# Rotary sine product moved ahead of the swap of halves, and two S5 tables moved to ScalarE, in a two-layer hybrid encoder

## The chip, the cores and the metric

The program runs on one core of a Trainium2 chip. The metric is the time of one execution on the device in microseconds (us), the median of several runs. TensorE is called PE here as in the profile, VectorE DVE, ScalarE ACT, GpSimd POOL and SyncE SP; SP computes nothing and issues most of the DMAs. PE writes its results to an accumulator memory (PSUM), from which DVE and ACT can read; all else lies in the main on-chip memory (SBUF).

## The reference, cut to what matters

Two layers over 1024 tokens of width 1024, each a mixer and an MLP. The change lies in the first mixer: a combined projection gives queries and keys (4 heads, two halves of 64 each), values, and the input of an S5 layer (32 groups of 16 channels, a complex diagonal state of 64 per group, in both directions). Queries and keys are rotated:

```
def apply_rope(t, cos, sin):
    t1, t2 = jnp.split(t, 2, axis=-1)
    return jnp.concatenate([t1 * cos - t2 * sin, t2 * cos + t1 * sin], axis=-1)
...
    q = apply_rope(split_qk(q), cos, sin) * (ATTN_QK_DIM ** -0.5)
    k = apply_rope(split_qk(k), cos, sin)
```

The S5 layer is a scan over time, whose step for one state is `ar`, `ai`, with the result read out through `c_re`, `c_im`:

```
    elems = (jnp.broadcast_to(ar, bur.shape), jnp.broadcast_to(ai, bur.shape), bur, bui)
    _, _, xr, xi = lax.associative_scan(_complex_affine_combine, elems,
                                        reverse=(direction == 1), axis=1)
```

## The kernel before

Activations lie transposed, 128 channels on the partitions and 1024 tokens along a row. A float32 product is done as three products of split halves (`mm_part`, L133): a tile of a projection is 48 matmuls of 128x512.

The first mixer has three parts in time. First the projections of the S5 input and the S5 parameters. Then, in `s5_main`, eight batches of four groups. Each batch has `s5_gains` (tables: `gtr`, `gti` by DVE and POOL, the rotation `wr`, `wi`, the decay `dec`, a transposed input `U`), `s5_readout` and `s5_kernels` (mostly POOL, ACT and small matmuls, ending in the Toeplitz tile `toep`, which eight DMAs spread from `KK`), `s5_states` (matmuls L824 into the accumulator `side`, then sixteen DVE instructions L827 to L853, four of them scans L838 and L841 that read `dec`) and `s5_out` (matmuls L864 to L866). The rotation is an angle in turns `fr` less its nearest whole number, then two sines on ACT: one of `fr` itself (L747) and one of a quarter turn less its absolute value (L748), which DVE takes (L746).

The twelve tiles of queries, keys and values come as "fill": `qk_tile` eight times and `val` four times. In the text of the program they stand behind the loop over the batches. What each engine does first is decided by a planner (`schedule_with_timeline_sim=True`), which orders the instructions of every engine by its own estimate of the times. So the matmuls of the fill lie between those of the batches. Once ordered, each engine works strictly in its order, and so does the DMA queue of SP.

A rotated tile goes through `qk_tile` so: ACT copies the accumulator `ps` with a scale to `raw` (tile `qraw`, L919); four DMAs swap blocks of 32 partitions into `sw` (L923); DVE multiplies `ps` by the cosine into `t` (tile `rot`, L925); POOL multiplies `sw` by the sine (L926); DVE adds (L927); ACT and DVE split the sum into `qh` and `ql` (L108, L109), which DMAs L931 and L932 store to DRAM. The last tile (i = 7) accumulates in `side`, the others in `big`. After the mixer's gated unit (`glu`), the attention loads queries, keys and values back (L957 to L961).

The accumulators are scarce: two `big`, one `side`, one `sm` and one `fill`. PE waits before a matmul until the tile that it overwrites has been read.

Of the kernel before, what the change touches and what calls it, by code (L numbers as in the profile page):

```python
# [13 lines left out]
AF = mybir.ActivationFunctionType  # L14
ALU = mybir.AluOpType
# [12 lines left out]
NB = 4  # L28
# [27 lines left out]
class Trunk:  # L56
# [661 lines left out]
    def s5_gains(self, b, S, pb, u_tok):  # L718

        nc = self.nc  # L720
        v, gp = nc.vector, nc.gpsimd
        gs = slice(NB * b, NB * b + NB)
        N4 = [P, NB, 128]
        GT = [P, NB, 8, 16]
        t0, t1 = (pb.tile(GT, F32, tag=f"tm{k}", name=f"tm{k}") for k in range(2))
        bbr, bbi = (x[:, gs, :].unsqueeze(2).to_broadcast(GT) for x in S["bb"])
        g7r, g7i = (x[:, gs, :].unsqueeze(3).to_broadcast(GT) for x in S["g7"])
        gtr = pb.tile(GT, F32, tag="gtr", name="gtr")
        gti = pb.tile(GT, F32, tag="gti", name="gti")
        self.cmul(gtr, gti, g7r, g7i, bbr, bbi, t0, t1, v, gp)  # L730
        G = []
        for j, src in enumerate((gtr, gti)):
            ps = self.small()
            for g in range(NB):
                nc.tensor.transpose(ps[:, 128 * g : 128 * g + 128], src[:, g].rearrange("p s m -> p (s m)"), self.ident)
            t = pb.tile(N4, F32, tag=f"G{j}", name=f"G{j}")
            nc.scalar.copy(t, ps.rearrange("p (g k) -> p g k", g=NB))
            G.append(t)

        tn = wr = pb.tile(N4, F32, tag="wr", name="wr", bufs=2)  # L740
        fr = wi = pb.tile(N4, F32, tag="wi", name="wi", bufs=2)
        for g in range(NB):
            nc.scalar.activation(fr[:, g], S["count"], AF.Copy, scale=S["psi"][:, NB * b + g : NB * b + g + 1])
        v.tensor_scalar(tn, fr, MAGIC, MAGIC, ALU.add, ALU.subtract)
        v.tensor_tensor(fr, fr, tn, ALU.subtract)
        v.scalar_tensor_tensor(tn, fr, -1.0, fr, ALU.mult, ALU.max)  # L746
        nc.scalar.activation(wi, fr, AF.Sin, scale=TURN)  # L747
        nc.scalar.activation(wr, tn, AF.Sin, scale=-TURN, bias=S["quarter"])  # L748
        dec = pb.tile(N4, F32, tag="dec", name="dec")
        gp.tensor_tensor(  # L750
            dec, S["edge"].unsqueeze(1).to_broadcast(N4), S["rho"][:, gs].unsqueeze(2).to_broadcast(N4), ALU.mult
        )
        U = pb.tile(N4, F32, tag="U", name="U", bufs=2)
        ps = self.small()
        for g in range(NB):
            o = 512 * (b % 2) + 128 * g
            nc.tensor.transpose(ps[:, 128 * g : 128 * g + 128], u_tok[:, b // 2, o : o + 128], self.ident)
        nc.scalar.copy(U, ps.rearrange("p (g c) -> p g c", g=NB))
        return dict(U=U, G=G, w=(wr, wi), dec=dec)
# [153 lines left out]
    def qk_tile(self, i, xg, pr, cosr, sinr, dst, last):  # L913

        nc = self.nc
        ps = self.proj(self.load_w(W_QK + i), xg, self.side() if last else None)
        raw = pr.tile([P, SEQ], F32, tag="qraw", name="qraw")
        scale = -0.125 if i % 2 == 0 else 1.0
        nc.scalar.activation(raw, ps, AF.Copy, scale=scale)  # L919
        sw = pr.tile([P, SEQ], F32, tag="sw", name="sw")  # L920
        for a in range(4):
            b = a ^ 1
            nc.sync.dma_start(sw[32 * a : 32 * a + 32], raw[32 * b : 32 * b + 32])  # L923
        t = pr.tile([P, SEQ], F32, tag="rot", name="rot")
        nc.vector.scalar_tensor_tensor(t, ps, scale, cosr, ALU.mult, ALU.mult)  # L925
        nc.gpsimd.tensor_tensor(sw, sw, sinr, ALU.mult)  # L926
        nc.vector.tensor_tensor(t, t, sw, ALU.add)  # L927
        hi = pr.tile([P, SEQ], F32R, tag="qraw", name="qh")
        lo = pr.tile([P, SEQ], F32R, tag="sw", name="ql")
        self.split(hi, lo, t)  # L930
        nc.sync.dma_start(dst[0], hi.bitcast(F32))  # L931
        nc.sync.dma_start(dst[1], lo.bitcast(F32))  # L932
# [581 lines left out]
def layout(i):  # L1514
    a = lambda k: np.asarray(i[k])
    mt = lambda w: w.reshape(8, 128, -1, 128).transpose(2, 1, 0, 3).reshape(-1, 128, 1024)

    def pairs(w, nk):
        m = w.reshape(-1, nk, 128, w.shape[1] // 256, 2, 128)
        return m.transpose(0, 3, 2, 4, 1, 5).reshape(-1, 128, 2 * nk * 128)  # L1520

    def blocks(w, ks, ms):

        t = w.reshape(-1, 128, w.shape[1] // 128, 128)
        return np.stack([t[k, :, m].transpose(1, 0, 2).reshape(128, -1) for m in ms for k in ks])

    halves = (list(range(4)), list(range(4, 8)))
    ffs = {}
    for l in range(2):
        win, wout = a("w_ff_in")[l], a("w_ff_out")[l]  # L1530
        ffs[f"win{l}"] = np.stack([blocks(win, halves, (2 * j, 2 * j + 1)) for j in range(16)])

        npairs = 16 - 2 * l
        parts = []
        for u in range(1, npairs + 4):
            rows = [[2 * j + f for j in range(max(0, u - 4), min(npairs, u))] for f in range(2)]
            q = (u - npairs) % 4
            parts.append(blocks(wout, rows, (q, q + 4)).ravel())
        ffs[f"wout{l}"] = np.concatenate(parts)
    ffs["wtail"] = np.stack([blocks(a("w_ff_out")[1], ([28, 29, 30, 31],), (d,))[0] for d in range(8)])  # L1540

    we = mt(a("w_in_even")[0])
    wqk = np.stack([we[0:4], we[4:8]], 1).reshape(8, 128, 1024)
    wo = mt(a("w_in_odd")[0]).reshape(5, 8, 128, 1024)
    odd = []
    for h in range(8):
        odd += [wo[0, h], wo[2, h], wo[3, h], wo[1, h], wo[4, h]]
    oo = a("w_out_odd")[0].reshape(8, 128, 1024)
    two = oo[5:7].reshape(2, 128, 8, 128)[:, :, PAIRED].reshape(2, 128, 2, 4, 128).transpose(2, 1, 3, 0, 4).reshape(2, 128, 1024)
    oo = np.concatenate([oo[:5], two, oo[7:]])  # L1550
    woe = a("w_out_even")[0]
    apart = woe[:512].reshape(4, 128, 2, 4, 128).transpose(3, 1, 2, 0, 4).reshape(4, 128, 1024)
    w = np.concatenate([
        we[12:16], wqk, we[8:12], pairs(a("s5_w_glu")[0], 4), apart, pairs(woe[512:], 4), np.stack(odd), oo,
    ])
    col = lambda v: v.reshape(-1, 128).T
    vec = np.concatenate([
        col(a("norm_mix_g")), col(a("norm_mlp_g")), col(a("final_norm_g")), col(a("hgrn_norm_g")),
        col(a("hgrn_lb_logits")), col(a("s5_b_glu")), col(a("diff_subln_g")),
    ], axis=1)  # L1560
    vec = np.concatenate([vec, np.zeros((128, 80 - vec.shape[1]), np.float32)], axis=1)
    up = np.triu(np.ones((128, 128), np.float32))
    consts = np.concatenate([np.eye(128, dtype=np.float32), up, up.T, np.tile(np.arange(128, dtype=np.float32), (128, 1))], axis=1)
    x = a("x")[0].T.reshape(8, 128, 1024)
    gp = lambda v: v.transpose(0, 2, 1).reshape(128, 32)
    step = np.broadcast_to(a("s5_log_step")[0][:, :, None], (2, 32, 64))
    s5_par = np.stack([gp(a("s5_lam_re")[0]), gp(a("s5_lam_im")[0]), gp(step)], 1)
    gpm = lambda v: v.transpose(0, 2, 1, 3).reshape(128, 32, 16)
    s5_b = np.stack([gpm(a("s5_b_re")[0]), gpm(a("s5_b_im")[0])], 1)
    gpn = lambda v: v.transpose(0, 3, 1, 2).reshape(128, 32, 16)  # L1570
    s5_c = np.stack([gpn(a("s5_c_re")[0]), gpn(a("s5_c_im")[0])], 1)
    inv = 10000.0 ** (-np.arange(0, 64, 2, dtype=np.float32) / np.float32(64.0))
    ang = np.arange(SEQ, dtype=np.float32)[None, :] * inv.astype(np.float32)[:, None]
    cos, sin = np.cos(ang).astype(np.float32), np.sin(ang).astype(np.float32)
    cos = np.tile(cos, (4, 1))
    sin = np.tile(np.concatenate([-sin, sin]), (2, 1))
    lam = np.broadcast_to(a("diff_lambda")[0], (128, 4, 64))
    s5_d = a("s5_d")[0].reshape(32, 16).T
    return {"w": w, "vec": vec, "consts": consts, "x": x, "s5_par": s5_par, "s5_b": s5_b, "s5_c": s5_c, "s5_d": s5_d,
            "cos": cos, "sin": sin, "lam": lam, **ffs}  # L1580
# [18 lines left out]
```

## Time and profile before

| What | Value |
|---|---|
| median of 3 runs | 2706.62 us (2703.37, 2706.62, 3588.91) |
| the profiled execution | 2711.57 us, its span 2709.7 us |
| granted PE clock, mean of the span | 0.97 |
| PE busy | 2511.2 us (93%) |
| DVE busy | 2021.5 us (75%) |
| ACT busy | 1055.7 us (39%) |
| POOL busy | 920.9 us (34%) |

The profiled execution is 4.95 us above the median, and 1.87 us of it lie outside its span. PE's busy share is high nearly everywhere; the stretches in which it is not are few, and the one that the change touches lies between 60 and 375 us.

### The profile page before, as it was taken

To read this page: it belongs to the slowest core of one execution; us is meant where nothing else is said; L and a number is where in the kernel's file an instruction comes from. 1 tells how busy PE (TensorE), PEld (TensorE's weight loads), DVE (VectorE), ACT (ScalarE), POOL (GpSimd) and SP (SyncE) were. 2 spreads that over 40 slices of the span, in tenths; PEclk is the share of its full clock that TensorE was granted. 3 is DMA by queue.
4 is the path that set the end of the run, shared out by engine and by line. 5 is a ranking of instruction groups with operands and counts; after the bars stand their busy time and mean duration, and the time that the engine had idled before them with its cause. 6 is when DMAs were issued, how large, how long until landed. Compare 5 with 4: busy or idle time off the path is not lost.

```text
span 2709.7 us, 33309 instructions
## 1 busy us (share of the span) xinstructions
PE 2511.2 (93%) x12040; PEld 2074.6 (77%) x12040; DVE 2021.5 (75%) x2896; ACT 1055.7 (39%) x1911; POOL 920.9 (34%) x732
## 2 busy tenths in 40 slices
PE   6888889998999989999799999999978999899987
PEld 5767768886788867777688888888857888678776
DVE  9688867868667678887876766666677676688867
ACT  3333346665334344444421222222254343444434
POOL 6455421213332334453222222222223323344422
PEclk9898999998999989999899999999989999999999
DMA  3122362302334356666111111111122343466672
GB/s 145 59 77 79 128 179 63 90 28 98 96 113 127 103 150 147 161 172 172 37 45 39 40 40 39 40 39 40 51 78 75 114 124 114 135 152 170 149 190 75
DMA packets 135253, 269.02 MB, mean 99 GB/s; under 512 B 16432, under 2 KB 29360, under 8 KB 135088
## 3 DMA queue, kind: packets, MB, share of 16 engines
q1 hardware_dynamic: 118384, 236.47, 27.2%
q0 software_dynamic: 16704, 30.42, 7.2%
q8 instruction: 95, 1.56, 0.2%
q14 instruction: 70, 0.57, 0.1%
HBM read 173.50 MB, written 87.03 MB: 96 GB/s over the span
## 4 chain that ended last, share of the span: by engine, by line
PE 57%; DVE 22%; DMA 8%; issue 7%; ACT 2%; POOL 2%; SPq 1%; POOLq 0%; DVEq 0%; ACTq 0%
PE big L133 21%; PE b L352 10%; PE c L352 6%; PE a L352 6%; DMA z<-sq 5%; DVE wl L109 4%; DVE l L109 3%; PE sm L1010 2%; PE sm L133 1%; PE big L1379 1%; PE tail L542 1%; ACT h L108 1%; PE big L975 1%; PE sm L1335 1%; PE big L1350 1%
## 5 line engine op out<-in xcount | busy, mean ns | idle before, releaser
L133 PE MATMUL big<-hi,wh 128*128 128x512 f32 x976 | 310.1, 398 | 13.7 <-ACT hi L111 12.1
L133 PE MATMUL big<-lo,wh 128*128 128x512 f32 x976 | 308.2, 395 | 9.7 <-DVE lo L112 9.7
L133 PE MATMUL big<-hi,wl 128*128 128x512 f32 x976 | 307.3, 395 | 0.0
L352 PE MATMUL b<-h,wh 128*128 128x512 f32 x672 | 270.4, 402 | 30.2 <-DVE w L362 23.6
L352 PE MATMUL b<-h,wl 128*128 128x512 f32 x672 | 267.1, 398 | 2.5 <-DVE wl L109 2.5
L352 PE MATMUL b<-l,wh 128*128 128x512 f32 x672 | 266.8, 397 | 0.3 <-DVE l L109 0.3
L108 ACT CAST wh<-s 128x512 fp32r<-128x512 f32 (+3 forms) x204 | 118.6, 583 | 343.5 <-PE b L352 170.0
L109 DVE TENSOR_TENSOR l<-z,h 128x512 fp32r<-128x512 f32 x232 | 196.0, 873 | 75.2 <-ACT h L108 74.8
L109 POOL TENSOR_TENSOR wl<-raw,wh 128x1024 fp32r<-128x1024 f32 x58 | 143.0, 2466 | 317.1 <-ACT wh L108 308.3
L108 ACT CAST wh<-raw 128x1024 fp32r<-128x1024 f32 x74 | 77.5, 1047 | 436.0 <-PE big L133 295.6
L133 PEld LDWEIGHTS big<-lo,wh 128*128 128x128 f32 x976 | 184.6, 190 | 49.7 <-DVE lo L112 11.0
L133 PEld LDWEIGHTS big<-hi,wh 128*128 128x128 f32 x976 | 182.2, 190 | 52.5 <-ACT hi L111 12.8
L109 DVE TENSOR_TENSOR wl<-r,wh 128x512 fp32r<-128x512 f32 (+3 forms) x279 | 215.5, 780 | 8.7 <-ACT wh L108 8.6
L133 PEld LDWEIGHTS big<-hi,wl 128*128 128x128 f32 x976 | 184.7, 190 | 38.5 <-issue 0.2
L108 ACT CAST h<-z 128x512 fp32r<-128x512 f32 x232 | 139.3, 618 | 179.3 <-DMA z<-sq 76.0
L108 ACT CAST wh<-r 128x512 fp32r<-128x512 f32 (+3 forms) x279 | 158.7, 581 | 99.6 <-PE b L352 46.5
L352 PE MATMUL a<-h,wh 128*128 128x512 f32 x448 | 178.1, 398 | 14.1 <-ACT wh L108 7.5
L352 PE MATMUL c<-h,wh 128*128 128x512 f32 x448 | 177.4, 396 | 10.2 <-ACT h L108 7.8
L326 POOL TENSOR_TENSOR s<-s,r 128x512 f32<-128x512 f32 (+3 forms) x68 | 98.6, 1450 | 252.0 <-DVE wl L109 251.0
L333 POOL TENSOR_TENSOR s<-s,r 128x512 f32<-128x512 f32 (+3 forms) x68 | 89.9, 1323 | 273.2 <-DVE wl L109 224.2
L352 PE MATMUL a<-h,wl 128*128 128x512 f32 x448 | 177.1, 395 | 5.3 <-DVE wl L109 5.3
L352 PEld LDWEIGHTS b<-h,wh 128*128 128x128 f32 x672 | 128.6, 191 | 68.9 <-DVE w L362 33.5
(438 smaller groups left out, 6025.4 us busy)
## 6 DMA issues: line engine op xcount, KB each, us to landing
raw<-w SPq DMA_DIRECT2D x74, 512.0 KB, 3.3
r<-win SPq DMA_DIRECT2D x128, 256.0 KB, 3.0
sq<-z SPq DMA_DIRECT2D x128, 256.0 KB, 3.0
z<-sq SPq DMA_DIRECT2D x128, 256.0 KB, 4.9
xd<-z POOLq DMA_DIRECT2D x116, 256.0 KB, 5.8
r<-wout SPq DMA_DIRECT2D x96, 256.0 KB, 4.6
x<-x SPq DMA_DIRECT2D x16, 512.0 KB, 7.6
xd<-x SPq DMA_DIRECT2D x32, 256.0 KB, 2.3
```

The costliest lines, as they stand in the source:

```text
L108: nc.scalar.copy(hi, src)
L109: (eng or nc.vector).tensor_tensor(lo, src, hi, ALU.subtract)
L133: nc.tensor.matmul(ps[:, t], a[:, s], b[:, t], start=(first and i == 0 and j == 0), stop=(last and i == n - 1 and j == 2),)
L326: gp.tensor_tensor(s2, s1, r["r11"], ALU.add)
L333: gp.tensor_tensor(s2, s2, r["r12"], ALU.add)
L352: nc.tensor.matmul(bank[p], x[:, s], y, start=(p in (1, 6, 5) and i == 0 and j == 0), stop=(i == n - 1 and j == 2), skip_group_check=True,)
L542: nc.tensor.matmul(ps, x[:, ks], y, start=(k == 0 and j == 0), stop=(k == 3 and j == 2))
L975: nc.tensor.matmul(S[:, ks], qa[:, qs], kk[:, ks], start=True, stop=False)
L1010: nc.tensor.matmul(po, wT[:, k, :], A["V"][:, k, :], start=(k == 0), stop=(k == NT - 1))
L1335: nc.tensor.matmul(ps[:, 128 * b : 128 * b + 128], ki[:, bs], qd[:, bs], start=True, stop=True)
L1350: nc.tensor.matmul(kv[:, bs], kTs[d][:, bs], V[:, bs], start=True, stop=True)
L1379: nc.tensor.matmul(po[:, bs], l, r, start=(i == 0), stop=(i == len(terms) - 1))
```

## The change

In `s5_gains` the absolute value moves from DVE (L746) to ACT, and the decay table `dec` from POOL (L750) to ACT, where it becomes four instructions of 128 columns. In `qk_tile` the product with the sine is taken from the accumulator by DVE, ahead of the swap, in place of ACT's copy; POOL's product behind the swap goes. The host's sine table has its signs exchanged to fit.

```diff
@@ s5_gains
-        v.scalar_tensor_tensor(tn, fr, -1.0, fr, ALU.mult, ALU.max)
+        nc.scalar.activation(tn, fr, AF.Abs)
...
-        gp.tensor_tensor(
-            dec, S["edge"].unsqueeze(1).to_broadcast(N4), S["rho"][:, gs].unsqueeze(2).to_broadcast(N4), ALU.mult
-        )
+        for g in range(NB):
+            nc.scalar.activation(dec[:, g], S["edge"], AF.Copy, scale=S["rho"][:, NB * b + g : NB * b + g + 1])
@@ qk_tile
-        nc.scalar.activation(raw, ps, AF.Copy, scale=scale)
+        nc.vector.scalar_tensor_tensor(raw, ps, scale, sinr, ALU.mult, ALU.mult)
...
         nc.vector.scalar_tensor_tensor(t, ps, scale, cosr, ALU.mult, ALU.mult)
-        nc.gpsimd.tensor_tensor(sw, sw, sinr, ALU.mult)
         nc.vector.tensor_tensor(t, t, sw, ALU.add)
@@ layout
-    sin = np.tile(np.concatenate([-sin, sin]), (2, 1))
+    sin = np.tile(np.concatenate([sin, -sin]), (2, 1))
```

The planner sees other instructions and orders the first mixer with its attention anew, and a short piece of the first MLP. Below, the line numbers of the changed kernel are 1 less than before from L754 to L925 and 2 less from L927 on; its new instructions are L746 (absolute value), L751 (decay) and L918 (sine product).

DVE around the seventh rotated tile, before: the tile's product and sum (L925, L927) stand behind the end of a batch, next to each other.

```order
L853 TENSOR_TENSOR z_1711<-z_1711,z_1710 128x512
L852 TENSOR_TENSOR z_1709<-z_1709,z_1712 128x512
L925 SCALAR_TENSOR_TENSOR rot<-big,cosr 128x1024
L927 TENSOR_TENSOR rot<-rot,sw 128x1024
L804 TENSOR_TENSOR d_1813<-d_1813,side 16x64
L806 TENSOR_TENSOR KK<-d_1813,d_1814 16x4x16
L109 TENSOR_TENSOR ql<-rot,qh 128x1024
```

The same tile on DVE after:

```order
L805 TENSOR_TENSOR KK<-d_1692,d_1693 16x4x16
L744 TENSOR_SCALAR wr<-wi 128x512
L745 TENSOR_TENSOR wi<-wi,wr 128x512
L918 SCALAR_TENSOR_TENSOR qraw<-big,sinr 128x1024
L924 SCALAR_TENSOR_TENSOR rot<-big,cosr 128x1024
L109 TENSOR_TENSOR wl<-raw,wh 128x1024
L826 TENSOR_TENSOR z_1730<-side,wr 128x512
L827 TENSOR_TENSOR z_1731<-side,wi 128x512
L828 TENSOR_TENSOR z_1732<-side,wr 128x512
L829 TENSOR_TENSOR z_1733<-side,wi 128x512
L775 SCALAR_TENSOR_TENSOR hi<-hi,tm_1814 128x640
L925 TENSOR_TENSOR rot<-rot,sw 128x1024
```

The sum (now L925) has moved away from the two products, behind a weight split and the first four instructions of the next batch; the end of the batch before it (`KK`) stands three rows ahead of the products.

The DMA queue of SP ahead of that tile's swap, before: the swap stands behind the store of a value tile.

```order
L809 DMA toep<-KK 16x4x128 x8
L116 DMA raw<-w 128x1024
L1133 DMA dv_123<-vtok 128x1024
L923 DMA sw<-qraw 32x1024 x4
L1478 DMA x_2775<-x 128x1024
```

And after:

```order
L116 DMA raw<-w 128x1024
L1131 DMA dv_123<-vtok 128x1024
L808 DMA toep<-KK 16x4x128 x8
L922 DMA sw<-qraw 32x1024 x4
L116 DMA raw<-w 128x1024
```

The eight Toeplitz DMAs have moved from ahead of a weight load to right ahead of the swap.

ACT in the third batch of tables, before: the copy of `U` stands behind the four angle instructions L743.

```order
L1132 COPY vtok<-fill 128x512
L743 ACTIVATE wi<-count,psi 128x128 x4
L758 COPY U<-sm 128x512
L1132 COPY vtok<-fill 128x512
L747 ACTIVATE wi<-wi 128x512
L748 ACTIVATE wr<-wr,quarter 128x512
```

And after:

```order
L788 COPY bz_800<-bk_600 64x4x16
L1130 COPY vtok<-fill 128x512
L746 ACTIVATE wr<-wi 128x512
L747 ACTIVATE wi<-wi 128x512
L757 COPY U<-sm 128x512
L748 ACTIVATE wr<-wr,quarter 128x512
```

The copy of `U` (now L757) has moved behind the absolute value and the first sine.

## Rows read from the trace of the kernel before

**Rows 1.** Busy time by stretch: span, then PE, PEld, DVE, ACT, POOL, granted clock, DMA.
```profile
100.00:354.00 254.00, 217.78 (x1127) 182.24 (x1125) 218.74 (x224) 88.12 (x158) 135.85 (x110) 0.92 0.31 100
354.00:405.00 51.00, 42.14 (x181) 34.04 (x182) 26.73 (x27) 25.28 (x30) 9.64 (x4) 0.91 0.63 166
405.00:600.00 195.00, 191.47 (x1226) 169.11 (x1226) 146.98 (x235) 128.57 (x288) 37.99 (x36) 1.00 0.24 60
```

**Rows 2.** PE's waits from 100 to 358 us: total us, times, longest.
```profile
PE sm L865 <- DVE z L852: 13.0, 4, 4.5
PE side L824 <- DVE d L804: 10.3, 3, 4.0
PE sm L864 <- ACT U L758: 7.8, 3, 4.1
PE fill L1131 <- DVE rot L1125: 2.3, 1, 2.3
PE side L133 <- DVE z L830: 1.8, 1, 1.8
```

**Rows 3.** Busy time by slices of 10 us around one wait of PE.
```profile
200.00:210.00 10.00, 7.13 (x28) 5.99 (x29) 9.70 (x13) 4.91 (x14) 2.82 (x3) 0.66 0.50 161
210.00:220.00 10.00, 8.91 (x56) 7.58 (x56) 6.42 (x5) 5.48 (x7) 7.33 (x4) 1.00 0.31 105
```

**Rows 4.** DVE by form, 100 to 375 us: busy, mean ns, idle before.
```profile
L927 DVE TENSOR_TENSOR rot<-rot,sw 128x1024 f32<-128x1024 f32 x8 | 11.8, 1469 | 12.4 <-POOL sw L926 9.6 <-DMA toep<-KK 2.7
...
L925 DVE SCALAR_TENSOR_TENSOR rot<-big,cosr 128x1024 f32<-128x1024 f32 x7 | 8.5, 1216 | 3.8 <-ACT qraw L919 3.8
...
L746 DVE SCALAR_TENSOR_TENSOR wr<-wi 128x512 f32<-128x512 f32 x6 | 4.1, 691 | 0.2
```

**Rows 5.** POOL by form, same stretch.
```profile
L926 POOL TENSOR_TENSOR sw<-sw,sinr 128x1024 f32<-128x1024 f32 x8 | 20.5, 2566 | 18.1 <-DMA sw<-qraw 18.1
...
L750 POOL TENSOR_TENSOR dec<-edge,sp 128x512 f32<-128x512 f32 x7 | 9.2, 1313 | 0.6
```

**Rows 6.** DVE in order of time, four pieces: start, us, instruction.
```profile
133.25 1.23 DVE L925 SCALAR_TENSOR_TENSOR rot<-big,cosr 128x1024 f32<-128x1024 f32 x1
...
137.21 2.83 DVE L849 TENSOR_TENSOR z<-z,wr 128x512 f32<-128x512 f32 x1
...
140.10 0.67 DVE L850 TENSOR_TENSOR z<-z,wi 128x512 f32<-128x512 f32 x1
...
283.36 2.88 DVE L610 TENSOR_TENSOR gtr<-g,bbr 128x512 f32<-128x512 f32 x1
...
322.10 1.53 DVE L849 TENSOR_TENSOR z<-z,wr 128x512 f32<-128x512 f32 x1
...
368.72 1.23 DVE L927 TENSOR_TENSOR rot<-rot,sw 128x1024 f32<-128x1024 f32 x1 [3.02 <-POOL sw L926]
```

**Rows 7.** POOL in order of time, first two tiles.
```profile
116.27 2.38 POOL L926 TENSOR_TENSOR sw<-sw,sinr 128x1024 f32<-128x1024 f32 x1 [3.48 <-DMA sw<-qraw]
...
133.45 1.04 POOL L750 TENSOR_TENSOR dec<-edge,sp 128x512 f32<-128x512 f32 x1
...
136.70 2.79 POOL L926 TENSOR_TENSOR sw<-sw,sinr 128x1024 f32<-128x1024 f32 x1
```

**Rows 8.** ACT in order of time, first tile.
```profile
110.87 1.03 ACT L919 ACTIVATE qraw<-big 128x1024 f32<-128x1024 f32 x1 [3.32 <-PE big L133]
```

**Rows 9.** The DMA queue of SP in order of time, sixth tile.
```profile
272.90 5.96 SPq L809 DMA_DIRECT2D toep<-KK  x8
278.98 2.46 SPq L923 DMA_DIRECT2D sw<-qraw  x4
```

**Rows 10.** ACT by form, 100 to 375 us.
```profile
L743 ACT ACTIVATE wi<-count,psi 128x128 f32<-128x128 f32 x24 | 7.7, 389 | 40.2 <-DVE z L851 40.2
...
L747 ACT ACTIVATE wi<-wi 128x512 f32<-128x512 f32 x6 | 3.8, 630 | 4.5 <-DVE wr L746 4.4
```

**Rows 11.** PE in order of time, start of the attention.
```profile
389.45 0.47 PE L975 MATMUL big<-kk,qa 128*128 128x512 f32 x1 [1.81 <-DMA kk<-dk]
```

## The prediction

> **What bounds the kernel now.** I began with the share of busy time by stretch, because an average over 2710 us says little about a change that touches 300 of them. From 100 to 354 us, in which the S5 batches and the fill run together, PE and DVE are each busy 86% of the time (217.8 and 218.7 of 254 us); ACT has 35% and POOL 53% [rows 1]. Behind it, in the attention, PE is busy 98% at full clock. So the stretch to read is the first one, and both of its busy engines count.
>
> Next, PE's waits there. The large ones add up to 35.2 us, of which 27.4 end with DVE (the last instructions of a batch's states, the small sum `d`, a scaled value tile, the reads of `side`) and 7.8 with ACT, a copy of `U` out of the only `sm` accumulator [rows 2]. PE never waits for POOL. What PE waits for is therefore mostly a DVE that comes late, and POOL matters only through DVE.
>
> Each wait has a second price: in the 10 us in which PE waited 4 us, the granted clock was 0.66, and 1.00 in the next [rows 3]. Over the whole stretch it was 0.92 [rows 1], which is 0.08 x 254 = 20 us of work that the lower of the two levels (1.2 against 2.4 GHz) did not do.
>
> POOL reaches DVE in two ways. DVE waited 12.4 us for the sum of the rotation, nearly all of it behind POOL's sine product [rows 4]. And DVE's instructions with two operands in SBUF grow when POOL computes beside them: one that takes 0.67 us took 2.83 beside the 2.79 us sine product, others 2.88 and 1.53 [rows 6, 7]. An instruction with one operand in the accumulator does not grow: the cosine product took 1.23 us beside `dec` [rows 6, 7].
>
> **The change part by part, up to 354 us.** Seven of the eight rotated tiles lie there, the eighth behind.
>
> The sine product on DVE: seven times the price of its twin, the cosine product, 1.216 us [rows 4]: +8.5 us of DVE. It reads the accumulator, so I add no growth beside POOL. The accumulator is not held longer: the cosine product waited for ACT's copy before (3.8 us in sum [rows 4]), so the two reads followed each other then, 1.03 + 1.22 us, and do so now, 1.22 + 1.22. The Trainium skill (PSUM — Partial Sum Buffer, PSUM bank collisions raise a hardware error) says that two engines must not touch one bank at once, and the trace agrees, since the 3.8 us of waiting are that order. Had the two reads been able to overlap, putting both on DVE would have held each accumulator 1.2 us longer, 9.7 us in eight tiles; by that rule there is no such overlap to lose.
>
> The absolute value leaves DVE: six times 0.691 us in the stretch [rows 4]: -4.1 us.
>
> POOL's two products go. In order of time I find four of the eight sine products beside a DVE instruction that grew by 2.2 us (2.83 and 2.88 against 0.67 [rows 6] are two of them) and six of the seven `dec` beside one that grew by 0.86 (1.53 against 0.67 is the last). So 4 x 2.2 + 6 x 0.86 = 14.0 us of DVE come back. Net DVE work: 8.5 - 4.1 - 14.0 = -9.6 us.
>
> The waits for the sum: 12.4 us before, of which 3.0 belong to the last tile [rows 4, 6]; -9.4 us. In their place DVE itself now waits for the swap. From the end of ACT's copy to POOL's start took 111.90 to 116.27, 4.4 us, in the first tile [rows 7, 8]. The new order puts other work between the products and the sum. In the first tile it is the cosine product, a sum of 640 columns and a weight split, 1.2 + 0.8 + 1.2, so 1.2 us are left. In the fifth and the seventh the Toeplitz DMAs have come ahead of the swap in the queue of SP; eight of them took 6.0 us and the swap began behind them [rows 9]. From `KK` on the queue needs 6.0 + 4.4 = 10.4 us, and DVE has two instructions of 512 columns, three of 1024, four of 512 and one of 640 to do, 1.4 + 3.6 + 2.7 + 0.8 = 8.5 us; 2 us are left, twice. The other four tiles have 5 us or more between and none left. New waits 1.2 + 2 + 2 = 5.2 us; net -4.2 us, with ends at -9.4 and, if a late queue strikes three tiles more at 2 us, 11.2 - 9.4 = +1.8.
>
> DVE gains 9.6 + 4.2 = 13.8 us. What of it is PE's? At most the share of PE's waits that DVE ends, 27.4 of 35.2, or 0.78 [rows 2]; but what is late next is ACT and PE itself, which are both nearly as far behind. I take 0.6: -8.3 us, ends -10.8 and -3.
>
> ACT loses seven copies of 1.03 us [rows 8] and gets six absolute values, priced as the sine of the same width at 0.630, and the decay in four pieces of 0.389, 1.56 us per batch [rows 10]. In sum that is some 7 us more, on an engine that idles 65% of the stretch, and it waited 40.2 us ahead of the angle instructions alone [rows 10]. It costs where it stands ahead of the copy of `U`: three waits of PE end there [rows 2], at most 3 x (1.56 + 0.63) = 6.6 us. I take +1, because in most batches the planner put `dec` or the copy elsewhere.
>
> **Behind 354 us.** The last tile's chain loses POOL's 2.4 us and starts earlier, since all its matmuls now precede the last `s5_out`. It feeds the attention's loads, but PE has the gated unit to do meanwhile and waited 1.8 us for a key tile [rows 11]: -1, ends -1.8 and +1. The attention's order changes in every head; PE idles 3.5 us of 195 there [rows 1], so up to 3.5 can be won and, as an estimate, as much lost: 0. Shorter waits give back some clock: of the 20 us, at most the part that belongs to the waits saved, 10.8 / 35.2, or 6 us; I take -1, because a wait that is shortened is not gone.
>
> The sum: -8.3 + 1 - 1 - 1 = -9.3 us against the profiled execution, 2702.3. That execution lies 4.95 us above the median of the runs, so the median becomes 2706.62 - 9.3 = 2697 us.
>
> **The rivals.** *PE was the bound.* Its 86% and its own order set the stretch, and DVE's gain only turns into waits of DVE. For it: PE at reduced clock is busy or waiting all the time. Against it: 27.4 us of waits that end with DVE. It gives 0 to -3: 2705 us.
>
> *The swap takes POOL's place, slower than before.* DVE waits in its own order for a transfer that only POOL had waited for, 18.1 us in sum [rows 5], and everything behind it on DVE waits too: the scans, the reads of `side`, the splits of weights. If SP issues a swap as late as in the sixth tile, 6 us, DVE would have 5 us of cover against 10.4 and wait 5.4. At four such tiles beside the first, 4 x 5.4 + 1.2 = 22.8, the waits cost 22.8 - 9.4 = 13.4 and eat the 9.6 us of work; from there it is slower, and with 6.6 us on ACT it gives 3.8 + 6.6, taken at 0.6: +6, 2713 us. The order shows two tiles with the DMAs ahead, which speaks against four.
>
> *POOL took more than I count.* If every POOL product that goes gave DVE its whole length, 20.5 + 9.2 = 29.7 us [rows 5] in place of 14.0, DVE would gain 29.5 and PE 0.6 of it, 17.7: with the other terms 2688 us. The Trainium skill (SBUF — State Buffer, Who interferes with whom) calls the port that the two engines share an exclusive lock, held for a whole instruction while the other blocks; the trace agrees where both met (2.83 us) but four sine products met no such instruction, and that keeps this rival behind.
>
> *The change does nothing on the chip that it says*, such as a reload of ACT's tables for the absolute value. The order shows the same number of loads before and after.
>
> **How the numbers follow.** Forecast 0.50 (2697); PE was the bound 0.17 (2705); POOL took more 0.15 (2688); the swap 0.13 (2713); the rest 0.05. From 2683 (the ends -10.8, -6, -1.8 and -3.5 together give 2684.5) to 2711 I leave out most of the swap's case and the rest, under 0.2. Two per cent is about what a measurement of this kernel can tell from no change, and that is 54 us: more than all of PE's waits with their clock (35 + 20), so no case reaches it. Faster by over 2% 0.015, within 0.97, slower 0.015.
>
> **What would show it.** Right: between 100 us and the end of the batches DVE's busy time falls by some 10 us, with the first scans' and products' mean times lower; PE's waits for `z` and `d` fall from 23 to under 17 us; the sum of the rotation waits 5 to 8 us for the swap; the granted clock of the stretch is at or over 0.92. Wrong: DVE's waits for the swap beyond 12 us, waits of PE for `U` beyond 10 us, or an attention in which PE idles more than 7 us.

## The result, and the profile after

The changed kernel takes 2696.16 us in the median (9 runs, 2684.45 to 2705.39). Eight runs of the kernel before, timed beside it, took 2703.36 to 2716.07 us, 2709.3 in the median; a ninth, of 3588.91 us, fell in a slower state of the chip and is left out. The ratio is 0.9945 with a 95% interval of 0.993 to 0.9959: a small change, but clear of the noise, which lies well under the 2% that the prediction took for it. The forecast was 2697 us. The profiled execution took 2696.16 us with a span of 2694.4 us, 15.3 us less than the span before.

The forecast of the time was met to 1 us, but in part by luck. It set a fall of 9.3 us against a median of 2706.62 us; the fall from profile to profile is 15.3, and the kernel before itself came out at 2709.3 when it was timed again. The fall was also made of other parts than forecast. To see them I use one mark, the last start of the matmuls of `s5_out`, which ends the S5 stretch. The rows, before and then after (first and last start stand ahead of the semicolon):

```profile
L866 PE MATMUL sm<-hi,z x64: 274/421/422, 143.0 to 358.2; 128*128 128x128 f32 x64
```

```profile
L865 PE MATMUL sm<-hi,z x64: 275/275/422, 137.0 to 336.6; 128*128 128x128 f32 x64
```

The stretch ends 21.6 us earlier, more than twice what was forecast; the end of the program only 15.3. A mark is one profiled execution's. Three edits below (a buffer more for the keys, in either kernel, and one for the decay) leave the order of PE and DVE up to the mark as it was; their marks lie 0.2 to 1.7 us from their kernel's, so a difference of 2 us says little. Busy time by stretch after (span, then PE, PEld, DVE, ACT, POOL, granted clock, DMA): the S5 stretch, the way to the attention, the attention. They answer to [rows 1].

```profile
100.00:337.00 237.00, 213.78 (x1140) 178.76 (x1138) 204.61 (x223) 94.02 (x184) 108.59 (x96) 0.95 0.34 109
337.00:381.00 44.00, 35.81 (x157) 28.26 (x158) 25.18 (x26) 22.69 (x27) 4.84 (x2) 0.92 0.71 192
381.00:577.00 196.00, 186.17 (x1197) 166.69 (x1195) 140.80 (x233) 125.46 (x289) 35.26 (x36) 0.98 0.23 57
```

The same window before, from 100 us to its mark:

```profile
100.00:358.00 258.00, 221.66 (x1147) 186.12 (x1146) 218.80 (x224) 88.12 (x158) 135.85 (x110) 0.91 0.31 98
```

Nearly the same number of matmuls stands in both windows. DVE is busy 14.2 us less, PE 7.9 us less at a clock of 0.95 in place of 0.91, and 13.1 us of PE's idle time are gone (36.3 to 23.2). In the attention PE, busy 98% before, has 95% (186.17 of 196 us).

PE's waits from 100 to 337 us after, which answer to [rows 2]:

```profile
PE sm L864 <- DVE z L851: 8.8, 4, 6.7
PE side L823 <- DVE d L803: 8.2, 5, 3.1
PE fill L1129 <- DVE rot L1123: 3.0, 2, 2.2
...
PE sm L863 <- ACT U L757: 0.9, 2, 0.5
```

`z` and `d` fell from 23.3 to 17.0 us, and the copy of `U`, which I had expected to come later, all but vanished as a cause: 7.8 to 0.9.

DVE by form, 100 to 340 us (busy, mean ns, idle before), beside [rows 4]:

```profile
L925 DVE TENSOR_TENSOR rot<-rot,sw 128x1024 f32<-128x1024 f32 x8 | 9.7, 1216 | 6.4 <-DMA sw<-qraw 6.4
L918 DVE SCALAR_TENSOR_TENSOR qraw<-big,sinr 128x1024 f32<-128x1024 f32 x7 | 8.5, 1219 | 9.4 <-DMA dv<-vtok 5.3 <-PE big L133 4.1
L924 DVE SCALAR_TENSOR_TENSOR rot<-big,cosr 128x1024 f32<-128x1024 f32 x7 | 8.5, 1213 | 0.0
```

The sine product costs what its twin costs. The sum, both of whose operands lie in SBUF, fell from a mean of 1469 ns to 1216: before, two of the eight took 2.28 and 2.14 us beside POOL's products for the S5 tables (four others met POOL's instructions and took no longer than alone), and after none did. That fall is mostly a matter of the order, for with POOL's sine products all but gone in the order of before (below) the mean is still 1466. The products from the accumulator never grew, 1.20 to 1.23 us each, also beside POOL. The Trainium skill (SBUF — State Buffer, Who interferes with whom) says that a DVE instruction with two operands in SBUF contends with a POOL instruction that reads SBUF, and one with at most one such operand (outside the two-port modes) doesn't; these times agree.

### The profile page after: what moved, and what is told of

Read it like the earlier page. It is cut to its first block, busy times and chain, and to the rows that moved or that the text cites. A ratio compares the mean times of both kernels' runs of the same rounds, so it can differ in the third digit from the quotient of the medians.

```text
span 2694.4 us, 33291 instructions
## 1 busy us (share of the span) xinstructions
PE 2511.5 (93%) x12040; PEld 2078.9 (77%) x12040; DVE 1989.8 (74%) x2896; ACT 1059.7 (39%) x1943; POOL 894.6 (33%) x716
## 3 DMA queue, kind: packets, MB, share of 16 engines
q1 hardware_dynamic: 118384, 236.47, 27.4%
q8 instruction: 95, 1.56, 0.2%
## 4 chain that ended last, share of the span: by engine, by line
PE 61%; DVE 14%; DMA 6%; issue 6%; ACT 2%; POOL 2%; SPq 1%; POOLq 0%; DVEq 0%; ACTq 0%
PE big L133 21%; PE b L352 12%; PE c L352 8%; PE a L352 8%; DMA z<-sq 4%; DVE wl L109 3%; DVE l L109 2%; PE sm L1008 2%; PE big L1377 1%; PE sm L133 1%; PE tail L542 1%; PE sm L1333 1%; PE big L1348 1%; PE big L973 1%; DMA xd<-z 1%
## 5 line engine op out<-in xcount | busy, mean ns | idle before, releaser
L133 PE MATMUL big<-hi,wh 128*128 128x512 f32 x976 | 311.4, 398 | 11.5 <-ACT hi L111 11.5
L109 DVE TENSOR_TENSOR wl<-r,wh 128x512 fp32r<-128x512 f32 (+3 forms) x279 | 212.3, 769 | 8.6 <-ACT wh L108 8.3
L326 POOL TENSOR_TENSOR s<-s,r 128x512 f32<-128x512 f32 (+3 forms) x68 | 98.8, 1453 | 257.0 <-DVE wl L109 255.9
L352 PE MATMUL a<-l,wh 128*128 128x512 f32 x448 | 177.5, 396 | 2.5 <-DVE l L109 2.5
```

The source lines that it names most:

```text
L109: (eng or nc.vector).tensor_tensor(lo, src, hi, ALU.subtract)
L133: nc.tensor.matmul(ps[:, t], a[:, s], b[:, t], start=(first and i == 0 and j == 0), stop=(last and i == n - 1 and j == 2),)
L326: gp.tensor_tensor(s2, s1, r["r11"], ALU.add)
L352: nc.tensor.matmul(bank[p], x[:, s], y, start=(p in (1, 6, 5) and i == 0 and j == 0), stop=(i == n - 1 and j == 2), skip_group_check=True,)
```

## The experiments

All were timed in five rounds beside the kernel before. The table gives for each the ratio, the mark, PE's and DVE's busy time from 100 us to the mark, PE's waits there as the sum of the rows that end with DVE and with ACT, and the attention from the first score to the last product with the values. Before and after stand first.

| Kernel | Ratio, interval | Mark | PE | DVE | PE waits: DVE, ACT | Attention |
|---|---|---|---|---|---|---|
| before | 1 | 358.2 | 221.7 | 218.8 | 27.4, 8.9 | 207.6 |
| after | 0.9945 (0.993 to 0.9959) | 336.6 | 213.8 | 204.6 | 20.4, 2.5 | 214.4 |
| rotary part alone | 1.0059 (1.0045 to 1.0074) | 361.5 | 220.8 | 220.3 | 30.2, 10.9 | 215.2 |
| both tables alone | 1.0013 (0.9997 to 1.0028) | 357.8 | 220.1 | 211.7 | 13.2, 19.9 | 214.0 |
| absolute value alone | 0.9997 (0.9985 to 1.0008) | 356.2 | 217.4 | 212.7 | 27.8, 10.8 | 208.5 |
| decay alone | 1.0067 (1.005 to 1.0085) | 368.7 | 220.2 | 227.0 | 29.4, 17.4 | 218.7 |
| before, sine product narrow | 0.9951 (0.9934 to 0.9967) | 344.9 | 217.1 | 209.5 | 21.7, 6.1 | 209.4 |
| the same, sine work on DVE | 0.9978 (0.9968 to 0.9989) | 348.7 | 217.9 | 215.2 | 22.7, 8.3 | 204.7 |
| after, POOL's work put back | 0.9977 (0.9965 to 0.9989) | 347.8 | 214.0 | 220.9 | 27.3, 6.4 | 209.5 |
| after, another order | 0.9954 (0.994 to 0.9967) | 344.7 | 214.9 | 213.9 | 16.9, 12.9 | 211.9 |
| after, two decay buffers | 0.9928 (0.9909 to 0.9948) | 336.8 | 211.1 | 206.3 | 22.8, 2.9 | 214.6 |
| both tables, two decay buffers | 1.0017 (1.0005 to 1.0029) | 361.7 | 221.0 | 213.8 | 16.6, 19.5 | 213.5 |
| after, four key buffers | 0.991 (0.9895 to 0.9925) | 338.3 | 212.3 | 207.1 | 22.0, 3.5 | 205.9 |
| before, four key buffers | 0.9989 (0.9976 to 1.0002) | 357.2 | 220.1 | 218.6 | 27.1, 9.8 | 207.9 |

### The parts, each alone

My theory was that DVE's work decides and that the parts add up; the rival, that the planner's new order does. Four kernels, each with part of the diff, the rest as before.

The rotary part alone: the hunks of `qk_tile` and of the sine table.

```diff
-        nc.scalar.activation(raw, ps, AF.Copy, scale=scale)
+        nc.vector.scalar_tensor_tensor(raw, ps, scale, sinr, ALU.mult, ALU.mult)
...
-        nc.gpsimd.tensor_tensor(sw, sw, sinr, ALU.mult)
```

> Only the rotary part of the change; the absolute value and the decay stay where they were. The mark is the end of the last s5_out, which the whole change moved by -21.6 us (358.1 to 336.5 us). Theory 'work' (DVE gets back what POOL's products took from it, and parts add up): the sine product costs DVE 8.5 us and returns 8.8 and 4.2 us of waits, so DVE is 4 to 8 us better and the mark moves by -3 to -9 us. Theory 'order' (the gain comes from the planner's new order of PE and DVE, whatever the edit): the mark may move by anything between -20 and +10 us, and this run and the run of the two tables do not add up to -21.6 within 5 us.

Both tables alone, the absolute value alone and the decay alone: from `s5_gains`, both hunks, the first and the second.

```diff
-        v.scalar_tensor_tensor(tn, fr, -1.0, fr, ALU.mult, ALU.max)
+        nc.scalar.activation(tn, fr, AF.Abs)
...
-        gp.tensor_tensor(
...
+            nc.scalar.activation(dec[:, g], S["edge"], AF.Copy, scale=S["rho"][:, NB * b + g : NB * b + g + 1])
```

> Only the absolute value and the decay on ACT; the rotation stays on POOL. Theory 'work': DVE loses 4.1 us of its own and 5.2 us or more that dec took from it, and the mark (last s5_out) moves by -9 to -16 us. Theory 'order': anything between -20 and +10 us, and no sum with the rotary run. By either, waits of PE for U stay under 8 us.

> Only the absolute value on ACT. The order of PE is the same as before, instruction for instruction, and DVE's but for the eight that leave, so nothing here is the planner's. Theory 'work': DVE's busy time between 100 and 354 us falls by 4 to 5 us and the mark by 2 to 4 us, the time by 0 to 4 us. Theory 'order': the mark moves by less than 1.5 us, since the order stays.

> Only the decay on ACT, in four pieces of 0.39 us. Theory 'work': DVE gets back 5 us or more (the neighbours of the six dec products shrink from 1.5 to 0.7 us), and the mark moves by -3 to -9 us; with the run of the absolute value it adds up to the run of the two tables within 4 us. Theory 'order': it does not add up, and the mark may rise.

The parts do not add up. The mark moved by +3.3 us for the rotary part, by -0.4 for the tables and by +10.5 for the decay, where the theory of work had a fall for each; together the rotary part and the tables moved it by -21.6. No part alone makes the program faster, and two make it slower by 0.6 to 0.7%. PE's waits for `U`, which were to stay under 8 us by either theory, were 9.8 with the tables. The one part that left the order alone is the absolute value. Its mark moved by -2.0 us, at the edge of what was expected and hardly more than marks of one order differ, and the time by nothing measurable; of the 6.1 us that DVE is less busy in the window, 4.1 are the absolute values, and most of the rest is four instructions that no longer fall in it.

The tables alone show where a DVE that is 7 us freer can lead: PE's waits for DVE fell from 27.4 to 13.2 us, and those for ACT rose from 8.9 to 19.9. ACT in order of time there, ahead of the largest wait for `U` (idle before in brackets):

```profile
260.92 1.28 ACT L751 ACTIVATE dec<-edge,sp 128x128 f32<-128x128 f32 x4 [9.03 <-DVE z L840]
263.89 1.04 ACT L108 CAST qh<-rot 128x1024 fp32r<-128x1024 f32 x1 [1.69 <-issue]
264.84 1.04 ACT L108 CAST wh<-raw 128x1024 fp32r<-128x1024 f32 x1
265.79 0.58 ACT L757 COPY U<-sm 128x512 f32<-128x512 f32 x1
```

And PE:

```profile
266.42 0.80 PE L863 MATMUL sm<-toep,U 128*128 128x128 f32 x2 [5.88 <-ACT U L757]
```

The decay has one buffer, so it waits until DVE's last scan (L840) of the batch before has read it. On POOL the seven decays of the stretch idled 0.6 us in all [rows 5], and PE waited for POOL nowhere there [rows 2]. On ACT the decay stands 9.0 us in the queue, and `U` is the third instruction behind it.

### POOL's work taken away and put back, with the order fixed

To hold the order, these kernels are planned as usual, and then single instructions of the planned list are replaced or added, with their waits and signals kept. In the first, the kernel before, POOL's sine products shrink:

```diff
+            a, b, c = (p.bass_ap[:, 0:8] for p in (old.outs[0], *old.ins))
+            new = nc.gpsimd.tensor_tensor(a, b, c, ALU.mult)
...
+            body[k] = end.pop()
```

> The kernel before, in its own order, instruction for instruction; only POOL's eight sine products are cut to 8 of their 1024 columns after the order is fixed (so the queries and keys are left unrotated in the other columns). What is taken away is POOL's work there: 8.0 us of growth of DVE beside it and up to 9.4 us of waits for it. Theory 'work' (DVE's time is PE's at 0.6, as in the prediction): the mark, the last s5_out at 358.2 us before, comes 6 to 11 us earlier, and so does the end. Theory 'order' (the place of instructions in their queues decides, and PE's waits stand elsewhere): the mark moves by less than 4 us, PE's wait for U stays near 7.8 us.

The mark came 13.3 us earlier and the time fell by 0.5%: above the range of the theory of work, and far from the rival's 4. Until the mark:

```profile
100.00:345.00 245.00, 217.06 (x1142) 182.36 (x1140) 209.46 (x222) 87.61 (x156) 119.61 (x109) 0.93 0.32 104
```

DVE is busy 9.3 us less (8.8 had been counted for the sine products), and waited 3.2 us for the sum in place of 9.4: some 15.5 us of DVE's time against 13.3 of the mark, a share of 0.86.

In the second, the changed kernel gets POOL's work back where nothing waits for it:

```diff
+            new = nc.gpsimd.tensor_tensor(free[:, o : o + n], cos[:, 0:n], sin[:, 0:n], ALU.mult)
+            new.wait_op(handle, done, "sem-ge", check=False)
+            body.insert(k, end.pop())
```

> The changed kernel, its order unchanged up to the attention; after the order is fixed, POOL gets seven products of 1024 columns and seven of 512 back, without anything waiting for them, about where the sine products and the decays stood. Theory 'work': DVE grows by some 12 us beside them and the mark (336.6 us) comes 6 to 11 us later. Theory 'order': DVE grows as much, and the mark moves by less than 4 us, since the gain came from what stands ahead of what.

```profile
100.00:348.00 248.00, 214.04 (x1143) 177.41 (x1141) 220.93 (x224) 93.56 (x183) 141.33 (x110) 0.94 0.28 87
```

DVE grew by 16.3 us (204.61 to 220.93), and the mark came 11.2 us later, just past the top of the theory's range. PE's waits for `d` alone rose from 8.2 to 14.1:

```profile
PE side L823 <- DVE d L803: 14.1, 6, 5.2
```

One sum that met an added product on POOL took 3.15 us in place of 1.22:

```profile
113.84 3.15 DVE L925 TENSOR_TENSOR rot<-rot,sw 128x1024 f32<-128x1024 f32 x1 [1.31 <-DMA sw<-qraw]
```

So POOL's work beside DVE is a cause: taken away in the order of before, put back in the order of after. The first run takes DVE's wait for the product away too; in the second nothing waits, and POOL's computing alone moves the mark. The third run asks what the move to DVE costs, still in the order of before:

```diff
+            new = nc.vector.scalar_tensor_tensor(free[:, o : o + SEQ], old.ins[0].bass_ap, 1.0, sin, ALU.mult, ALU.mult)
...
+            body.insert(k, keep(new, old, False))
```

> The kernel before in its own order up to the attention. As in the run with the narrow sine products, POOL keeps 8 columns of them; in addition DVE does, ahead of each of the first seven products by the cosine, a product of the accumulator by the sine (1.22 us) that nothing uses. So the work is moved from POOL to DVE as in the run of the rotary part alone, in the order of before. Theory 'work, at 0.7 of DVE's time': the mark comes 5 to 8 us after that of the narrow run (344.9 us), at 350 to 353, some 7 us ahead of before; then the 361.5 us of the rotary part alone hold 8 to 12 us that are the planner's order. Theory 'the sine product holds the accumulator, or DVE was the bound all along': 353 to 358 or later, and the rotary part alone is explained without an order.

The mark stands at 348.7 us, 3.8 us behind the narrow run and 9.5 us ahead of before: a little better than the theory of work, and not near the rival. (The attention of this kernel began only 0.9 us ahead of before, at 383.9 us against 384.8, for a reason that was not looked into; the comparison goes by the mark.) The rotary part alone has the same work, but for ACT's copy of 1 us a tile, which it saves, and for the swap, which there follows DVE's product and not the copy; its mark is 361.5 us. Apart from that, the 12.8 us between them are what the planner's order cost there.

In the order of before the rotary part is thus worth 9.5 us of the mark and the absolute value 2.0. The other 10 of the 21.6 us belong to the decay, which no run prices in that order, and to the new order; the runs don't part them.

### The order alone

The changed kernel, planned as if POOL still had a product to do, which is then cut to 8 columns:

```diff
-        nc.vector.scalar_tensor_tensor(t, ps, scale, cosr, ALU.mult, ALU.mult)
+        nc.vector.scalar_tensor_tensor(t, ps, scale, cosr, ALU.mult, ALU.mult); nc.gpsimd.tensor_tensor(self.scr, cosr, sinr, ALU.mult)
...
+            a, b, c = (p.bass_ap[:, 0:8] for p in (old.outs[0], *old.ins))
+            new = nc.gpsimd.tensor_tensor(a, b, c, ALU.mult)
```

> The changed kernel in another order: the planner sees a product of POOL of 1024 columns beside each product by the cosine, and after the order is fixed that product is cut to 8 columns. What the engines do in the S5 stretch is the same as in the changed kernel but for eight instructions of about 0.1 us on POOL; only the order is different (some 280 rows of PE's). Theory 'work': the mark stays at 336.6 us within 3. Theory 'order': it moves by more than 5 us, to 342 to 355 if the changed kernel's order was a lucky one.

The same work in another order ends the stretch 8.1 us later, beyond the theory of work alone. PE's waits there:

```profile
PE sm L864 <- DVE z L851: 8.7, 3, 6.8
PE sm L863 <- ACT U L757: 6.3, 3, 4.7
PE fill L1129 <- ACT vtok L1130: 4.3, 1, 4.3
```

Waits for ACT are 12.9 us in place of 2.5. DVE, too, is busy 213.9 us in place of 204.6, in 227 instructions against 223. The four that fall in the window besides are some 2.4 us of it; for the other 7 us the same instructions took longer, so which of DVE's instructions stands beside which of POOL's is itself a matter of the order. Of the whole program the ratio shows less, 0.9954 against 0.9945, since this order's attention is 2.5 us shorter (211.9 us); the profiled spans differ by 6.1 us (2700.5 against 2694.4).

### The wait that came with the decay

Two buffers for the decay were to take ACT's wait away, in the changed kernel and in the one with both tables alone:

```diff
-        dec = pb.tile(N4, F32, tag="dec", name="dec")
+        dec = pb.tile(N4, F32, tag="dec", name="dec", bufs=2)
```

> The changed kernel with two buffers for the decay in place of one; the order of PE, DVE and ACT stays in the stretch. ACT then no longer waits for the scans of the batch before (some 28 us in seven waits) ahead of each decay. Theory 'ACT blocked in its queue costs PE only where the copy of U stands behind': here U costs 0.9 us, so the mark moves by 0 to -2 us. Rival 'the blocked ACT delays everything behind it': -3 to -8 us.

> The run of the two tables alone (absolute value and decay on ACT, rotation as before) with two buffers for the decay. There PE waited 9.8 us for U and 9.4 us for other copies of ACT, with the decay just ahead of U in ACT's queue, waiting up to 9 us for the scans. Theory 'ACT blocked': the waits for U fall under 4 us and the mark (357.8 us) comes 5 to 12 us earlier. Rival 'U is late for another reason' (the matmuls that it copies, or the order): the mark moves by less than 3 us.

Neither run tests what it was made for: the wait is still there. In the second, ACT ahead of the same copy of `U`:

```profile
260.41 1.28 ACT L751 ACTIVATE dec<-edge,sp 128x128 f32<-128x128 f32 x4 [6.64 <-DVE z L840]
261.71 1.05 ACT L108 CAST qh<-rot 128x1024 fp32r<-128x1024 f32 x1
262.67 1.04 ACT L108 CAST wh<-raw 128x1024 fp32r<-128x1024 f32 x1
263.61 0.58 ACT L757 COPY U<-sm 128x512 f32<-128x512 f32 x1
```

The planner used the second buffer to issue the decay of one more batch at the very start, so that each decay behind it belongs to a batch later and waits for the same scan. In the changed kernel ACT's decays waited 28.8 us in place of 28.6; the marks agree within 0.2 us, and the intervals of the ratios overlap. In the tables' kernel the planner ordered PE's matmuls anew besides, so that run compares two orders: PE's waits for `U` were 13.7 us (9.8 with one buffer), and the mark came 3.9 us later. That the decay's wait delays `U` was thus not confirmed by taking it away. But the traces show it grow and shrink with the wait. Ahead of the fourth batch's `U` in the stretch the decay idled 2.9 us after, and PE then waited 0.4 us for `U`; in the other order of the same work it idled 11.5, and PE waited 4.7:

```profile
200.17 1.28 ACT L751 ACTIVATE dec<-edge,sp 128x128 f32<-128x128 f32 x4 [11.53 <-DVE z L840]
201.46 1.04 ACT L108 CAST qh<-rot 128x1024 fp32r<-128x1024 f32 x1
202.42 0.58 ACT L757 COPY U<-sm 128x512 f32<-128x512 f32 x1
```

### The attention

The attention took 214.4 us after and 207.6 before. PE's waits for keys there were 4.6 us in two places, at changes of a head:

```profile
PE big L973 <- DMA kk<-dk: 4.6, 2, 2.6
```

A head has two sets of queries and keys, and with three buffers SP loads the next head's second set only when PE has read out the first set of the head that it is in. At the larger wait PE did the last scores with that set from 458.43 to 459.61 us. SP, which had waited 30.4 us for PE, began with the four loads of queries at 459.40, and the two of keys came behind them:

```profile
462.54 0.59 SPq L955 DMA_DIRECT2D kk<-dk  x1
463.17 0.59 SPq L956 DMA_DIRECT2D kk<-dk  x1
```

They landed 5.4 and 5.9 us after their issue, the second at 469.10 us. PE had no work left from 466.85 on:

```profile
469.45 0.76 PE L973 MATMUL big<-kk,qa 128*128 128x512 f32 x1 [2.60 <-DMA kk<-dk]
```

A fourth buffer lets SP load the keys one set ahead, so that the scores there wait for no keys. First in the changed kernel:

```diff
-            qa, qb, kk = (pa.tile([P, SEQ], F32R, tag=t, name=t, bufs=3) for t in ("qa", "qb", "kk"))
+            qa, qb, kk = (pa.tile([P, SEQ], F32R, tag=t, name=t, bufs=3 + (t == "kk")) for t in ("qa", "qb", "kk"))
```

> The changed kernel with four buffers for the keys in the attention in place of three; the order of PE and DVE stays, SP loads the keys of the next head earlier. From the first score to the last product with the values the attention took 207.6 us before and 214.4 us after. Theory 'the key load of the next head comes late at the change of a head' (PE waited 4.6 us for it after, 1.8 before): the attention takes 207 to 210 us and the time falls by 4 to 7 us. Rival 'the order of scores and products itself': 213 to 215 us, no difference in the time beyond 2 us.

The attention took 205.9 us, a little less than the theory's range, and no wait for keys is left. PE's idle time there fell by 5.7 us (15.8 to 10.1), a little more than the waits for keys; its busy time fell by 2.8 (198.6 to 195.8), at a granted clock of 0.98 in place of 0.97. Its window from the first score to the last product with the values:

```profile
364.10:570.00 205.90, 195.82 (x1246) 173.75 (x1245) 154.62 (x249) 135.69 (x300) 37.10 (x36) 0.98 0.27 71
```

The last product came 4.9 us earlier than after (570.0 against 574.9), though this execution began the attention 3.6 us later. The ratio of 0.991 lies below that of the change with no overlap of the intervals. It is the lowest of the study, though its interval overlaps that of the kernel with two decay buffers.

The same buffer in the kernel before:

> The kernel before with four buffers for the keys in place of three (the planner then orders the attention anew; the S5 stretch keeps its order). In the changed kernel the fourth buffer took the attention from 214.4 to 205.9 us. Theory 'the late key load is what the changed kernel's order brought': before had one wait of 1.8 us for keys, so the attention stays at 205 to 209 us and the time falls by 0 to 4 us. Rival 'a fourth buffer helps any order': the attention falls by 6 us or more, to under 202, and so does the time.

It took 207.9 us for the attention and 0.9989 of the time, an interval that holds 1. So the fourth key buffer was worth something in the order that ran into the load, and nothing measurable in the order that did not.

## Why the prediction was right, and where it wasn't

**DVE's work: -9.6 forecast, -14.2 measured.** The sine product (+8.5) was right to a tenth. The growth beside POOL was rightly found as the cause, and for the sine products rightly sized (8.8 counted, 9.3 measured in the order of before). Of the 4.6 us that were not forecast some may belong to the two products: put back in the order of after, they cost DVE 16.3 us, 2.3 more than the 14.0 counted. The rest is of a size with what an order alone does to DVE (some 7 us for the same instructions). The decay's share was not measured by itself. The eighth tile's products by sine and cosine, 2.4 us that I had put behind the stretch, lie in it after.

**The waits for the sum: -4.2 forecast.** The waits behind the swap came out as counted, even below (3.2 us in place of 5.2; DVE gave up 9.4), and in the tiles that were named: 1.3 us in the first, 1.5 in the fifth, 0.4 in the seventh. But I gave the sine product no wait of its own. It writes the tile `qraw`, whose buffer it shares with the value tiles, and stood 5.3 us for the store of one. With 4.1 us for PE, where the cosine product had waited 3.8, the net is 3.2 + 9.4 - 9.4 - 3.8 = -0.6. DVE's total of -14.8 agrees with the forecast of -13.8 by errors on both sides.

**The share of 0.6: -8.3 on PE.** PE's waits that end with DVE fell from 27.4 to 20.4, by 7.0 us. With the clock in it the share is higher, 0.86 by the narrow run. `z` and `d` fell to 17.0 us, just at the bound ("under 17") that the prediction set as a sign of being right.

**ACT: +1 forecast, -6.4 measured.** This step failed in its sign. I priced ACT's work by its length, and not by the waits that it takes away or brings. Before, the longest wait of PE for `U`, 4.1 us, stood behind a copy of ACT that the change takes away, and that copy had waited 6.3 us itself:

```profile
201.32 1.02 ACT L919 ACTIVATE qraw<-big 128x1024 f32<-128x1024 f32 x1 [6.32 <-DVE ql L109]
202.24 0.58 ACT L758 COPY U<-sm 128x512 f32<-128x512 f32 x1
```

The next longest, 3.3 us, stood behind the angle instructions L743, which had waited 8.5 us for DVE; in the order of after these four idle 3.9 us there and stand further ahead of `U`. Against these two, the decay brings along its wait for the scans of the batch before, 28.6 us in sum on ACT:

```profile
L751 ACT ACTIVATE dec<-edge,sp 128x128 f32<-128x128 f32 x28 | 9.0, 391 | 28.6 <-DVE z L840 28.6
```

Alone, the decay and the tables cost PE 8.5 and 11.0 us more behind ACT. With the rotary part this became a gain, and in another order of the same work it is again a loss (12.9 against 8.9 before). So the 6.4 us are a property of the change in the order that it got, not of the change alone.

**The clock: -1 forecast, -7.9 measured.** The mechanism of [rows 3] was right and the term mis-sized by far. PE's busy time in the window fell by 7.9 us, beyond even the 6 us that I gave as its bound. But it does not follow the waits: with POOL's work put back PE idled 10.8 us more behind DVE and ACT than in the changed kernel (33.7 against 22.9), and its busy time stayed at 214.0. The five kernels with the whole change have 211 to 215 us, the other nine 217 to 222. The traces' records of the granted clock say the same: from 100 us to the mark the five were at the lower level (1.2 GHz) three to six times, 19 to 27 us in sum, the nine seven or eight times, 34 to 44 us (before 44.3, after 23.8). What in the change holds the clock up stays open.

The three terms on PE, -7.0 - 6.4 - 7.9 = -21.3, make up the -21.6 of the mark, as they must: PE's time is busy or waiting.

**The attention: 0 forecast with ends at 3.5, +6.8 measured.** The rows behind 354 us were read for what idles there, 3.5 us, not for what a new order could run into; the load of the next head's keys had no slack. PE idled 15.8 us from the first score to the last product with the values, and 8.9 before (207.6 - 198.7): the 6.8 us are all waiting. Waits for keys are 2.8 of them (4.6 against 1.8); most of the others are longer waits for ACT, which no run tested. The prediction named "an attention in which PE idles more than 7 us" as a sign of being wrong; in a window like that of [rows 1], where it had 3.5, PE idled 9.8 of 196 us. From the mark to the first score 2.7 us were won where 1 was forecast, and behind the attention 2.2 were lost, which I did not look into.

So 2697 us was hit by an S5 stretch that gave more than twice what I said, an attention that took a third of it back, and a kernel before that had been timed 2.7 us low. The 15.3 us from span to span lie nearer to the rival "POOL took more than I count" (18.6) than to the forecast (9.3), but not by its mechanism: POOL's products gave DVE a little over half of their length (9.3 of 17.1 us), not the whole. "PE was the bound" is refuted by the narrow run, "the swap" by its 3.2 us. What I had left out is that the order is worth some 8 to 13 us in this stretch, as much as the work that was moved.

## What to carry to other kernels

Where a planner sets the order, an edit buys two things, its work and a new order, and a run of the edit alone measures their sum; hold the planned list fixed and replace single instructions in it to price the work, and plan the same work in another way to see what an order is worth. When work moves to another engine, move its waits in your account too: a buffer wait that costs nothing in one queue can hold up everything behind it in another. And follow a gain to the next stage: there a new order can run into the smallest slack, here in part one key buffer.

## What the runs showed of the hardware

POOL's product of 1024 columns takes some 2.6 us and one of 8 columns 0.43; cutting eight of them (20.5 to 3.4 us, 17.1 us of POOL) gave DVE 9.3 us of work back. Fourteen products that nobody waits for, 29.0 us on POOL, cost DVE 16.3:

```profile
L1603 POOL TENSOR_TENSOR cosr<-cosr,sinr 128x1024 f32<-128x1024 f32 x7 | 18.5, 2648 | 0.5
L1603 POOL TENSOR_TENSOR cosr<-cosr,sinr 128x512 f32<-128x512 f32 x7 | 10.5, 1502 | 0.6
```

In both cases that is a little over half of POOL's time, in stretches where DVE was busy some 85 to 90%. Four decays of 128 columns in a row on ACT, 0.39 us each, took 1.28 us together, less than their sum of 1.56.
